# A deeper u lead in layer 1, GpSimd splits in halves beside G, and adaLN tiles beside layer 0's routing

## The chip, the cores and the metric

One core of a Trainium2 chip runs the whole program. The metric is the device time of one execution in microseconds (us), as the median of several runs. The engines are PE (TensorE, matrix products), DVE (VectorE), ACT (ScalarE), POOL (GpSimd) and the DMA queues, of which SP issues most. Each engine works off its own list of instructions strictly in order; semaphores make one engine wait for another.

## The reference

The program is a two-layer transformer trunk for 256 latent and 256 context tokens of width 1024. Each layer has adaLN modulation, four token mixers, and an expert layer (PEER), which is the part that the change touches:

```
mod_lat = (jax.nn.silu(c) @ w_mod[l] + b_mod[l])[:, None, :]     # adaLN, six vectors per layer
...
def peer_ffn(h, w_q, subkeys, u, v):                             # 16384 experts of one neuron
    q = (x_t @ w_q).reshape(t, PEER_HEADS, 2, PEER_QDIM // 2)
    s = jnp.einsum('thpd,hpnd->thpn', q, subkeys)                # routing: scores of 2 x 128 keys
    s_top, i_top = lax.top_k(s, kk)
    ...
    best, pos = lax.top_k(cand, kk)                              # 16 experts per head and token
    g = jax.nn.softmax(best, axis=-1)
    a = jax.nn.gelu(jnp.einsum('td,thkd->thk', x_t, u_sel))
    return jnp.einsum('thk,thkd->td', g * a, v_sel)
```

Layer 0 treats latent and context tokens, layer 1 only the 256 latent ones.

## The kernel before

The expert layer doesn't gather. It multiplies the tokens with all 16384 rows of u, in 128 tiles of 128 experts, and later with all rows of v. A dense matrix G (experts x tokens), made from the routing's result, holds the weight of every expert for every token and is zero where an expert wasn't chosen. Layer 0 does this for 384 of its tokens and gathers rows for the last 128 (class `Chosen`, the indirect DMAs); layer 1 does it for all 256.

Products are made to float32 precision from split operands: a tile `raw` is loaded, ACT copies it into a rounded `w_hi` (L144), and DVE or POOL subtracts to get `w_lo` (L145). Three products, hi by hi, hi by lo and lo by hi, are added in PSUM (L183 for u, L806 for v). `lo_engine` gives a share of the subtractions, `self.share`, to POOL and the rest to DVE. There are two `w_hi` and two `w_lo` buffers, and 4 (layer 0) or 5 (layer 1) `raw` buffers.

A layer's expert part has these stages, in program order:

1. **Routing** (`route`): 16 products with w_q, scores, top-16 searches on DVE, one softmax (`g`, ACT's exponential at L984). Then `ahead()` emits the first `LEAD0` u tiles (`u_step`), whose results are parked in SBUF (`park`, ACT's gelu at L753). The routing's result is then transposed on PE (L998) into `i1T`, `i2T` and `gT`; these transposes are told to stand behind the last matmul of `ahead()`:

```
        last = ahead()
        for src, dst in ((e2[0], i1T), (e2[1], i2T), (g, None)):
            ps = self.psum("big")
            with self.tc.issue_after(last):
```

2. **Lead** (first loop of `experts`): the u tiles from `LEAD0` to `LEAD`, and between them the steps that make G (`g_step`, 48 in layer 0, 32 in layer 1). A step is three DVE operations on float16 (p2 L763, pg L767, p1 L771, shown as p, pg and p), 16 small products on PE (L779), ACT copies into `stage` (L782) and every other step a DMA of 1 MB to G in DRAM. The last `LEAD1` u tiles come after the last step.
3. **Experts** (second loop): G is read back (`gr`, L789), and for each of 128 tiles j the parked u result is multiplied with its rows of G (L795), split, and multiplied with v tile j (`v_step`). While u tiles are left, one follows each v step. So there are 128 minus `LEAD` steps with v and u, then `LEAD` steps with v alone.

In layer 0 the lead loop also calls `fill_in()`, which takes the next of 25 small steps that compute a part of layer 1's adaLN: 20 tiles of w_mod (a 512 KB load and 8 matmuls, L292) and five layouts (an ACT copy, four transposes on PE at L301, two or three tiny DVE operations at L305, L306 and L310).

The order of instructions on each engine isn't the program order. A scheduler plays the program through with modelled times and fixes each engine's list by that; the constants above and the place of a call in the program are what it starts from.

Of the kernel before, what the change touches and what calls it, by code (L numbers as in the profile page):

```python
# [8 lines left out]
F32 = mybir.dt.float32  # L9
# [26 lines left out]

GB = 16
GI = 8
LEAD = [40, 60]

LEAD0 = [17, 12]
LEAD1 = [6, 6]


# [10 lines left out]
MRAW1 = 5  # L55
MB = [2, 3]
SHARE = [0.64, 0.888, 0.75]
PSH = [[1.0, 0.65, 0.6], [1.0, 0.3, 0.3]]
GATHERS = [0.3, 2.35]
SHL = [0.3, 0.181]  # L60
DIRECT = 7
# [7 lines left out]
class K:  # L69
    def __init__(self, tc, a, out):  # L70
        self.tc, self.nc, self.a, self.out = tc, tc.nc, a, out
        self.n_lo = 0.0
        self.fresh = False
        self.gates = []
        self.rows = None
        self.fill = []
        self.share = 0.5


    def rsqrt(self, ss, inv_n):  # L80
# [57 lines left out]
                self.r = self.rsqrt(s["ps"][:, :n // 128], 1.0 / D)  # L138
        return step

    def split(self, hi, lo, src, lo_engine=None):

        nc = self.nc
        nc.scalar.activation(hi, src, AF.Copy)  # L144
        (lo_engine or nc.vector).tensor_sub(lo, src, hi.bitcast(F32))  # L145

    def lo_engine(self, work=1.0):

# [6 lines left out]
    def weights(self, src, n=1024, tag="w", whole=False):  # L155
        nc, pool = self.nc, self.wp if tag == "w" else self.wk
        raw = self.raw() if tag == "w" else pool.tile([128, n], F32, name="b_raw", tag="braw", bufs=BB)
        nc.sync.dma_start(raw, src)
        hi = pool.tile([128, n], F32R, name="w_hi", tag=tag + "hi", bufs=2 if tag == "w" else BB)
        lo = pool.tile([128, n], F32R, name="w_lo", tag=tag + "lo", bufs=2 if tag == "w" else BB)  # L160
        self.split(hi, lo, raw, self.lo_engine())
        return (hi, lo, raw) if whole else (hi, lo)

    def raws(self, name, n):
# [559 lines left out]
    def peer(self):  # L724
# [4 lines left out]
        tc, nc, a, l = self.tc, self.nc, self.a, self.l  # L729
        n = DENSE[l]  # L730
        nt = n // 128
        self.chosen = None
        lead = LEAD[l]
        with self.pool("pe") as hp, tc.tile_pool(name="gd", bufs=1, space=bass.MemoryType.DRAM) as dp:
# [13 lines left out]
            def u_step(j):  # L748
                hi, lo = self.weights(a["u"][l, j])
                ps = self.psum("acc")[:, :n]  # L750
                end = self.mm(ps, hi, lo, lambda kt: P[0][:, kt, :n], lambda kt: P[1][:, kt, :n], DT)
                park[j] = hp.tile([128, n], F32, name="park", tag="park", bufs=lead + 1)
                nc.scalar.activation(park[j], ps, AF.Gelu)  # L753
                if self.chosen:
                    self.chosen.behind = end.ins
                return end.ins
# [81 lines left out]
            def phase(i, ns):  # L838

                self.share, self.n_lo = PSH[l][i], 0.0  # L840
                if self.chosen:
# [4 lines left out]
            with self.pool("route") as wk:  # L846
                own = None
                if self.chosen:
                    own = wk.tile([128, DT, 128], F32, name="own")
                P[:] = self.norm_mod(wk, hp, NB, LAT if self.last else ALL, 1, n, own)  # L850
                self.share = SHARE[2]


                def ahead():
                    self.share, self.n_lo = PSH[l][0], 0.0
                    return [u_step(j) for j in range(LEAD0[l])][-1]

                self.route(wk, n, *P, own, i1T, i2T, gAB, ahead)
            with self.pool("rows") as p:
# [4 lines left out]
    def experts(self, l, lead, n, gp, vp, u_step, g_step, g_read, v_step, v_end, phase):  # L864

        tb = TB
        with self.pool("g") as p:
            gp.append(p)
            gather = phase(0, lead)
            k, k0, k1 = 0, LEAD0[l], lead - LEAD1[l]  # L870
            for i in range(k0, lead):
                u_step(i)
                gather()
                self.fill_in()
                while k < n // tb and k < (i + 1 - k0) * n / (tb * (k1 - k0)):
                    g_step(k * tb)
                    k += 1
            self.fill_in(99)
        with self.pool("v") as p:
            vp.append(p)  # L880
            g_read(0)
            gather = phase(1, 128 - lead)
            for j in range(128):
                if j == 128 - lead:
                    gather = phase(2, lead)
                if j % GI == 0 and j + GI < 128:
                    g_read(j + GI)
                v_step(j)
                if j + lead < 128:
                    u_step(j + lead)  # L890
                gather()
            if self.chosen:
                self.chosen.finish()
            v_end()
# [356 lines left out]
```

## Time and profile before

| | before |
|---|---|
| median of 3 runs | 3302.24 us (3292.46 to 3308.22) |
| profiled execution, its own time | 3292.48 us |
| span from first to last instruction | 3290.7 us |
| mean granted TensorE clock | 0.962 |
| layer 0: G made, first v product | 826.6 to 1027.4, 1051.8 us |
| layer 1: G made, first v product | 2530.8 to 2704.0, 2724.0 us |

The times inside the program are microseconds from the span's start. A view by windows tells how long each engine was busy in a stretch; the timeline lists single instructions, with the idle time before each and what ended it in brackets.

### The profile page before, as it was taken

The page shows a single profiled execution, that of the slowest core. Times are in us where ns is not written, and L with a number is a line of the kernel's source. Part 1 is how long each engine was busy: PE and PEld are TensorE (multiplying, and loading weights), DVE is VectorE, ACT ScalarE, POOL GpSimd, SP SyncE. Part 2 cuts the span into 40 slices and gives each one's busy share as a digit, 9 for nine tenths or more (in the row PEclk, how much of TensorE's full clock was granted, in tenths as well). Part 3 has the DMA queues.
Part 4 walks back from the last instruction along what each step waited for, and adds up shares of the span by engine and source line. Part 5 has one row for each costly group of instructions (what it writes and reads, how often), then busy time and mean ns, then how long its engine had stood idle before and what let it go on. Part 6 is the DMA issues. An engine that isn't in the chain of part 4 may idle for free. (4 is left out here: it accounts for less than half of the span.)

```text
span 3290.7 us, 49451 instructions
## 1 busy us (share of the span) xinstructions
PE 3074.5 (93%) x19063; PEld 2707.9 (82%) x19063; DVE 2361.8 (72%) x4092; ACT 1366.5 (42%) x2166; POOL 1527.7 (46%) x814
## 2 busy tenths in 40 slices
PE   7999999898887899999999997999987889999998
PEld 5877777797776799988899886788987888999887
DVE  5465453799986888787888875456599988666655
ACT  4454443323443333333333333355543544444454
POOL 1111322135443688877888862245345663222221
PEclk9999999899988999999999997899988999999999
DMA  7331332222668988888888865333434669666564
GB/s 253 106 103 46 112 113 98 72 91 90 249 231 273 306 304 293 292 279 299 295 295 282 274 209 175 116 122 130 149 120 135 211 216 303 211 215 209 191 194 133
DMA packets 251292, 641.21 MB, mean 195 GB/s; under 512 B 20016, under 2 KB 107696, under 8 KB 245936
## 3 DMA queue, kind: packets, MB, share of 16 engines
q1 hardware_dynamic: 208432, 461.88, 42.9%
q0 software_dynamic: 36864, 134.23, 11.7%
q10 hardware_dynamic: 5760, 41.95, 3.4%
q8 instruction: 149, 2.44, 0.3%
q14 instruction: 87, 0.71, 0.1%
HBM read 594.99 MB, written 42.99 MB: 194 GB/s over the span
## 5 line engine op out<-in xcount | busy, mean ns | idle before, releaser
L145 POOL TENSOR_TENSOR w_lo<-raw,w_hi 128x1024 fp32r<-128x1024 f32 x387 | 1008.7, 2611 | 1306.8 <-ACT w_hi L144 959.4
L144 ACT ACTIVATE w_hi<-raw 128x1024 fp32r<-128x1024 f32 x664 | 703.7, 1060 | 1168.4 <-PE ps_acc L183 468.1
L183 PE MATMUL ps_acc<-hhi,w_hi 128*128 128x256 f32 (+2 forms) x3136 | 988.5, 333 | 51.4 <-ACT park L753 19.8
L183 PE MATMUL ps_acc<-hlo,w_hi 128*128 128x256 f32 (+2 forms) x3136 | 964.6, 326 | 0.5 <-DVE hlo L355 0.5
L183 PEld LDWEIGHTS ps_acc<-hhi,w_hi 128*128 128x128 f32 x3136 | 611.4, 195 | 94.4 <-ACT park L753 21.2
L183 PEld LDWEIGHTS ps_acc<-hlo,w_hi 128*128 128x128 f32 x3136 | 608.8, 194 | 27.8 <-DVE hlo L355 1.5
L183 PE MATMUL ps_acc<-hhi,w_lo 128*128 128x256 f32 (+2 forms) x3136 | 576.5, 324 | 32.7 <-POOL w_lo L145 22.6
L183 PEld LDWEIGHTS ps_acc<-hhi,w_lo 128*128 128x128 f32 x3136 | 496.1, 192 | 62.2 <-POOL w_lo L145 26.7
L145 DVE TENSOR_TENSOR w_lo<-raw,w_hi 128x1024 fp32r<-128x1024 f32 x277 | 359.2, 1297 | 238.8 <-ACT w_hi L144 156.8
L806 PE MATMUL ps_big<-w_hi,whi 128*128 128x512 f32 x1280 | 341.6, 394 | 17.2 <-ACT w_hi L144 17.2
L806 PE MATMUL ps_big<-w_lo,whi 128*128 128x512 f32 x1280 | 332.9, 390 | 3.3 <-DVE w_lo L145 3.1
L806 PE MATMUL ps_big<-w_hi,wlo 128*128 128x512 f32 x1280 | 335.2, 391 | 0.0
L806 PEld LDWEIGHTS ps_big<-w_lo,whi 128*128 128x128 f32 x1280 | 239.4, 188 | 54.5 <-DVE w_lo L145 4.9
L806 PEld LDWEIGHTS ps_big<-w_hi,wlo 128*128 128x128 f32 x1280 | 240.9, 188 | 52.4
L806 PEld LDWEIGHTS ps_big<-w_hi,whi 128*128 128x128 f32 x1280 | 234.8, 189 | 57.3 <-ACT w_hi L144 18.9
L1100 DVE SCALAR_TENSOR_TENSOR ch<-row,cg,ch 128x1024 f32<-128x1024 f32 x127 | 232.3, 1829 | 68.7 <-DMA row<-in_v_rows,cx 67.6
L795 DVE TENSOR_TENSOR park<-park,gr 128x384 f32<-128x384 f32 (+1 forms) x256 | 232.8, 938 | 65.1 <-ACT park L753 37.6
L1094 DVE SCALAR_TENSOR_TENSOR row<-row,ch 128x1024 f32<-128x1024 f32 x128 | 211.8, 1670 | 77.2 <-DMA row<-in_u_rows,cx 76.7
L145 DVE TENSOR_TENSOR wlo<-park,whi 128x256 fp32r<-128x256 f32 (+1 forms) x214 | 203.0, 951 | 48.0 <-ACT whi L144 47.9
L1067 POOL DMA_INDIRECT row<-in_u_rows,cx x128 | 181.6, 1419 | 34.0 <-issue 18.3
L1067 POOL DMA_INDIRECT row<-in_v_rows,cx x128 | 174.8, 1366 | 30.5 <-issue 22.4
L753 ACT ACTIVATE park<-ps_acc 128x384 f32<-128x384 f32 (+1 forms) x256 | 110.6, 432 | 120.5 <-PE ps_acc L183 117.9
(223 smaller groups left out, 3469.6 us busy)
## 6 DMA issues: line engine op xcount, KB each, us to landing
raw<-in_u SPq DMA_DIRECT2D x256, 512.0 KB
raw<-in_v SPq DMA_DIRECT2D x256, 512.0 KB
raw<-in_w_mod SPq DMA_DIRECT2D x96, 512.0 KB
G<-stage ACTq DMA_DIRECT2D x40, 1024.0 KB
raw<-in_w_gate SPq DMA_DIRECT2D x64, 512.0 KB
gr<-G SPq DMA_DIRECT2D x16, 1536.0 KB
raw<-in_w_in SPq DMA_DIRECT2D x40, 512.0 KB
raw<-in_w_q SPq DMA_DIRECT2D x32, 512.0 KB
```

Source lines behind the costliest of these rows:

```text
L144: nc.scalar.activation(hi, src, AF.Copy)
L145: (lo_engine or nc.vector).tensor_sub(lo, src, hi.bitcast(F32))
L183: end = nc.tensor.matmul(ps, w[:, kt * 128:kt * 128 + 128], x(kt), start=i == 0, stop=i == 3 * nk - 1)
L753: nc.scalar.activation(park[j], ps, AF.Gelu)
L795: nc.vector.tensor_mul(w3, w3, g)
L806: m = nc.tensor.matmul(vacc[0][t][d], x[:, t * 128:t * 128 + 128], y[:, d * 512:d * 512 + 512], start=first, stop=end)
L1067: dma = nc.gpsimd.indirect_dma_start(out=row, out_offset=None, in_=self.k.a["u_rows" if i < SLOTS else "v_rows"], in_offset=bass.IndirectO ...
L1094: nc.vector.scalar_tensor_tensor(row, row, 1.0, self.h, op0=OP.mult, op1=OP.mult, accum_out=self.dot[:, s:s + 1])
L1100: nc.vector.scalar_tensor_tensor(self.y, row, self.g[:, s:s + 1], self.y, op0=OP.mult, op1=OP.add)
```

## The change

Layer 1 gets 84 u tiles in its lead instead of 60, and 28 of them, instead of 12, are emitted in `ahead()`. For the tiles of `ahead()` every subtraction stays on POOL (share 1.0), but in layer 1's lead loop POOL's share falls from 1.0 to 0.55. While a lead loop runs, in both layers, a subtraction that goes to POOL is cut into two of 512 columns. And `ahead()` now calls `fill_in()` after each u tile, so that 17 of layer 0's 25 adaLN steps are emitted there (in layer 1 there is nothing to fill in).

```
-LEAD = [40, 60]
-LEAD0 = [17, 12]
+LEAD = [40, 84]
+LEAD0 = [17, 28]
-PSH = [[1.0, 0.65, 0.6], [1.0, 0.3, 0.3]]
+PSH = [[1.0, 0.65, 0.6], [0.55, 0.3, 0.3]]
...
-    def split(self, hi, lo, src, lo_engine=None):
+    def split(self, hi, lo, src, lo_engine=None, pieces=1):
         nc = self.nc
         nc.scalar.activation(hi, src, AF.Copy)
-        (lo_engine or nc.vector).tensor_sub(lo, src, hi.bitcast(F32))
+        n = lo.shape[1] // pieces
+        for i in range(pieces):
+            c = slice(i * n, i * n + n)
+            (lo_engine or nc.vector).tensor_sub(lo[:, c], src[:, c], hi[:, c].bitcast(F32))
...
-        self.split(hi, lo, raw, self.lo_engine())
+        e = self.lo_engine()
+        self.split(hi, lo, raw, e, self.pieces if e is nc.gpsimd else 1)
...
                 def ahead():
-                    self.share, self.n_lo = PSH[l][0], 0.0
-                    return [u_step(j) for j in range(LEAD0[l])][-1]
+                    self.share, self.n_lo = 1.0, 0.0
+                    for j in range(LEAD0[l]):
+                        last = u_step(j)
+                        self.fill_in()
+                    return last
...
             k, k0, k1 = 0, LEAD0[l], lead - LEAD1[l]
+            self.pieces = 2
             for i in range(k0, lead):
...
             self.fill_in(99)
+            self.pieces = 1
```

No instruction of PE, ACT or SP is added or removed. Of the subtractions of full tiles, 12 move from POOL to DVE, and 53 of those that stay on POOL become 106 halves.

What moves is seen in the lists of the engines. First ACT in layer 1, from the softmax's exponential (`g<-g`) to the copies of the transposed routing (`i1T`, `i2T`, `gT`). Before (the numbers of tiles are shown, since the rows read alike without them):

```order
L984 ACTIVATE g_23229<-g_23229 128x256
L753 ACT_TABLE_LOAD
L753 ACTIVATE park_23685<-ps_acc_23660 128x256
L144 ACTIVATE w_hi_23836<-raw_23834 128x1024
L753 ACTIVATE park_23745<-ps_acc_23720 128x256
L144 ACTIVATE w_hi_23896<-raw_23894 128x1024
L753 ACTIVATE park_23805<-ps_acc_23780 128x256
L144 ACTIVATE w_hi_23929<-raw_23927 128x1024
L1002 ACTIVATE i1T_21968<-ps_big_23632 128x256
```

and in the changed kernel (L995 is L984, L145 is L144, L759 is L753 and L1013 is L1002 of before):

```order
L995 ACTIVATE g_23252<-g_23252 128x256
L759 ACT_TABLE_LOAD
L759 ACTIVATE park_23686<-ps_acc_23661 128x256
L145 ACTIVATE w_hi_23756<-raw_23754 128x1024
L759 ACTIVATE park_23719<-ps_acc_23694 128x256
...
L145 ACTIVATE w_hi_24267<-raw_24265 128x1024
L759 ACTIVATE park_24181<-ps_acc_24156 128x256
L1013 ACTIVATE i1T_21991<-ps_big_24183 128x256
```

Three parks stand between the exponential and the first transposed copy before, 16 after; ahead of the exponential 12 parks and 13 `w_hi` copies stand behind the routing's last `q`, in both. The first half of the added tiles is not placed beside the searches but behind the softmax.

Second, POOL in layer 1, from the routing's last conversion (`xf`) to its third subtraction in the expert stage (`wlo<-park`). Before:

```order
L940 CAST xf<-idx 128x32
L145 TENSOR_TENSOR w_lo<-raw,w_hi 128x1024 x46
L145 TENSOR_TENSOR wlo<-park,whi 128x256
L145 TENSOR_TENSOR w_lo<-raw,w_hi 128x1024 x21
L145 TENSOR_TENSOR wlo<-park,whi 128x256
```

and in the changed kernel:

```order
L951 CAST xf<-idx 128x32
L149 TENSOR_TENSOR w_lo<-raw,w_hi 128x1024 x15
L149 TENSOR_TENSOR w_lo<-raw,w_hi 128x512 x60
L149 TENSOR_TENSOR wlo<-park,whi 128x256
L149 TENSOR_TENSOR w_lo<-raw,w_hi 128x1024 x20
```

So 30 of the 56 lead tiles are split on POOL, in 60 halves; the rest are on DVE, 21 of them between its first and last operation for G. On PE, 45.75 u tiles lie between the first and the last product for G, where 33.5 lay before; 3.25 (before 3.2) lie between the transposes and the first of these products, and 6.7 between the last one and the first v product, in both.

Third, the SP queue at the end of layer 0's lead (`raw<-in_u`, `raw<-in_v` and `raw<-in_w_mod` are loads of tiles, `gr<-G` the reads of G). Before:

```order
L158 DMA raw<-in_u 128x1024
L289 DMA raw<-in_w_mod 128x1024 x2
L789 DMA gr<-G 128x24x128 x2
L158 DMA raw<-in_v 128x1024
L158 DMA raw<-in_u 128x1024
```

and in the changed kernel:

```order
L162 DMA raw<-in_u 128x1024 x16
L162 DMA raw<-in_v 128x1024
L162 DMA raw<-in_u 128x1024
L162 DMA raw<-in_v 128x1024
L162 DMA raw<-in_u 128x1024
L162 DMA raw<-in_v 128x1024
L162 DMA raw<-in_u 128x1024
L162 DMA raw<-in_v 128x1024
L795 DMA gr<-G 128x24x128 x4
```

Four v tiles and three u tiles are now asked for ahead of the first read of G, and no tile of w_mod stands near it. Of the 20 tiles of w_mod, 14 and three layouts now stand on PE ahead of layer 0's transposes, and ACT has 6 parks instead of 4 between layer 0's exponential and its transposed copies.

## Rows read from the trace of the kernel before

**Rows 1.** The page's busy times: engine, busy us, share of the span, instructions.

```profile
PE 3074.5 (93%) x19063; PEld 2707.9 (82%) x19063; DVE 2361.8 (72%) x4092; ACT 1366.5 (42%) x2166; POOL 1527.7 (46%) x814
```

**Rows 2.** Windows: stretch, busy us of the engines, granted clock, DMA share, GB/s.

```profile
2530.00:2704.00 174.00, 147.92 (x1392) 144.06 (x1391) 169.91 (x98) 84.66 (x138) 109.83 (x38) 0.96 0.59 203
...
2724.00:3111.00 387.00, 385.35 (x2463) 350.83 (x2462) 264.07 (x281) 185.91 (x274) 107.15 (x44) 1.00 0.71 225
3111.00:3273.00 162.00, 162.00 (x717) 134.07 (x715) 85.26 (x95) 78.85 (x115) 41.07 (x22) 1.00 0.55 177
...
827.00:1027.00 200.00, 165.96 (x1523) 151.81 (x1521) 181.40 (x172) 82.65 (x140) 81.75 (x29) 0.91 0.65 237
...
1052.00:1110.00 58.00, 47.72 (x215) 41.75 (x216) 44.10 (x57) 15.77 (x21) 33.54 (x21) 0.91 1.06 339
```

**Rows 3.** Timeline of layer 1's softmax, ACT (start, us, instruction, idle before).

```profile
2517.53 0.42 ACT L984 ACTIVATE g<-g 128x256 f32<-128x256 f32 x1 [8.15 <-DVE g L983]
...
2527.65 0.38 ACT L1002 ACTIVATE i1T<-ps_big 128x256 f16<-128x256 f32 x1
```

**Rows 4.** The same stretch on PE.

```profile
2519.69 0.58 PE L183 MATMUL ps_acc<-hhi,w_hi 128*128 128x256 f32 x1 [6.28 <-ACT park L753]
```

**Rows 5.** Timeline of DVE at the start of layer 1's G.

```profile
2530.79 0.68 DVE L763 TENSOR_TENSOR p<-iotaT,i2T 128x1024 f16<-128x1024 f16 x1
2531.39 3.43 DVE L771 TENSOR_TENSOR p<-iota,i1T 128x1024 f16<-128x1024 f16 x1
...
2544.33 1.21 DVE L767 TENSOR_TENSOR pg<-p,gAB 128x2048 f16<-128x2048 f16 x1
```

**Rows 6.** The same stretch on POOL.

```profile
2531.28 2.45 POOL L145 TENSOR_TENSOR w_lo<-raw,w_hi 128x1024 fp32r<-128x1024 f32 x1 [1.02 <-ACT w_hi L144]
```

**Rows 7.** Groups by line, 2530 to 2704: busy us, mean ns, idle before.

```profile
L145 POOL TENSOR_TENSOR w_lo<-raw,w_hi 128x1024 fp32r<-128x1024 f32 x38 | 112.5, 2965 | 64.8 <-ACT w_hi L144 42.9 <-PE ps_acc L183 14.2 <-ACT stage L782 7.8
...
L767 DVE TENSOR_TENSOR pg<-p,gAB 128x2048 f16<-128x2048 f16 x32 | 56.2, 1760 | 2.2 <-PE ps_big L779 2.2
...
L779 PE MATMUL ps_big<-p,pg 128*128 128x128 f16 x512 | 40.7, 237 | 26.1 <-DVE p L771 22.1 <-DVE pg L767 4.0
```

**Rows 8.** Timelines of DVE and of PE at the end of layer 1's lead.

```profile
2700.91 1.21 DVE L771 TENSOR_TENSOR p<-iota,i1T 128x1024 f16<-128x1024 f16 x1
...
2724.03 1.09 PE L806 MATMUL ps_big<-w_hi,whi 128*128 128x512 f32 x4
```

**Rows 9.** Groups of the whole run: POOL's half-wide split, DVE's full split.

```profile
L145 POOL TENSOR_TENSOR w_lo<-b_raw,w_hi 128x512 fp32r<-128x512 f32 x24 | 31.4, 1313 | 76.7 <-ACT w_hi L144 67.9 <-PE ps_big L607 8.3 <-issue 0.3
...
L145 DVE TENSOR_TENSOR w_lo<-raw,w_hi 128x1024 fp32r<-128x1024 f32 x277 | 359.2, 1297 | 238.8 <-ACT w_hi L144 156.8 <-PE ps_acc L183 74.9 <-PE ps_big L806 4.1
```

**Rows 10.** Timelines of POOL and DVE where a half-wide split met a DVE split.

```profile
53.76 1.29 POOL L145 TENSOR_TENSOR w_lo<-b_raw,w_hi 128x512 fp32r<-128x512 f32 x1 [0.33 <-ACT w_hi L144]
...
54.15 1.45 DVE L145 TENSOR_TENSOR w_lo<-b_raw,w_hi 128x512 fp32r<-128x512 f32 x1
```

**Rows 11.** Groups by line, 827 to 1045 (layer 0's lead).

```profile
L767 DVE TENSOR_TENSOR pg<-p,gAB 128x2048 f16<-128x2048 f16 x48 | 66.2, 1383 | 17.2 <-PE ps_big L779 17.2
...
L144 ACT ACTIVATE w_hi<-raw 128x1024 fp32r<-128x1024 f32 x21 | 22.1, 1056 | 26.5 <-DMA raw<-in_u 23.9 <-PE ps_acc L183 2.2 <-ACT stage L782 0.4
...
L292 PE MATMUL ps_big<-raw,cv 128*32 128x128 f32 x320 | 15.0, 306 | 0.0
```

**Rows 12.** Timelines of SP, DVE and PE where layer 0's G is read back.

```profile
1034.59 5.36 SPq L789 DMA_DIRECT2D gr<-G  x2
1040.04 5.54 SPq L158 DMA_DIRECT2D raw<-in_v  x1
...
1044.03 3.84 DVE L795 TENSOR_TENSOR park<-park,gr 128x384 f32<-128x384 f32 x8 [2.59 <-DMA gr<-G]
...
1051.75 1.65 PE L806 MATMUL ps_big<-w_hi,whi 128*128 128x512 f32 x3 [10.81 <-ACT w_hi L144]
```

More of the change, by code (lines that the diff above doesn't have):

```diff
@@ L878, in experts @@
             self.fill_in(99)
+            self.pieces = 1
         with self.pool("v") as p:
```

## The prediction

> **What bounds the kernel now.** The page comes first: PE is busy for 93% of the span [rows 1], so a change can win only where PE idles. The windows show where that is. While layer 1's experts run, PE has no gap, with v and u (387 us for 68 steps) or v alone (162 us for 60) [rows 2]. While layer 1's G is made, 2530 to 2704, PE is busy for 148 of 174 us and DVE for 170; in layer 0's lead PE for 166 and DVE for 181 of 200 [rows 2]. So DVE sets the pace of both leads, and the change moves PE work into them.
>
> The second thing to see is what DVE's time in layer 1's lead is made of. Alone, p2 takes 0.68 us, and pg and p1 1.21 us each; an operation starts some 0.08 us before the one in front of it ends [rows 5, 8]. But a p1 of 1.21 us took 3.43 when a POOL split had begun 0.1 us before it [rows 5, 6]. From the first p2 (2530.8) to the end of the last p1 (2702.1) [rows 5, 8] it is 171.3 us. The 32 steps alone are 32 x (0.60 + 1.13 + 1.13) = 91.5, and DVE waited 2.2 for PE [rows 7]; the other 77.6 us are stalls beside 38 POOL splits [rows 7], 2.04 us for each, 0.83 of a split's 2.45 [rows 6].
>
> The Trainium skill's page "SBUF — State Buffer", section "Who interferes with whom", says that a DVE instruction with two SBUF inputs and a GpSimd instruction that reads SBUF exclude each other, and that whoever issues first keeps the port for its whole instruction. By that rule the DVE splits that the change adds stand under the same lock, and the two engines' times would add up in full: 91.5 + 25.6 + 56 x 1.31 + 2.2 = 192.7 us on DVE in the stage worked out below, and v at 2784, where the share of 0.83 gives 180.3 us and, as far as DVE goes, v at 2772. The trace agrees with the lock [rows 5, 6], and with its holding for a DVE split too [rows 10].
>
> **Layer 1: what leaves the experts.** A step with v and u takes 387/68 = 5.69 us, one with v alone 162/60 = 2.70 [rows 2], so a u tile is worth 2.99 us there. 24 of them leave: -71.8 us.
>
> **Layer 1: the first 16.** ACT stood 8.15 us in front of the softmax's exponential, which waits for DVE's searches, and ran it at 2517.5; PE idled 6.28 us behind ACT until 2519.7 [rows 3, 4]. In the changed lists 12 parks stand ahead of the exponential, as before, so nothing more can run beside the searches, and PE's gaps up to 2519.7 stay. Behind it stand 16 parks instead of 3, and the transposes come behind the last of these tiles. 13 more tiles at 2.99 us push the transposes back by 38.9 us: the first copy from 2527.7 to 2566.6, the first p2 from 2530.8 to 2569.7 [rows 3, 5]. For these 39 us DVE has nothing to do. PE can hold 2.99 us there, since ACT's copy takes 1.06 us per tile [rows 11] and POOL's split 2.45 [rows 6]. If the tiles did fit beside the searches, this cost would be nothing; the list speaks against it.
>
> **Layer 1: while G is made.** DVE: 91.5 us for the steps; 21 splits, by their mean of 1.30 less 0.08 [rows 9], 25.6; and the stalls beside the 28 other tiles of this stage (of 3.25 + 45.75), split on POOL in 56 halves. The trace has no half of this tile in this stage. Its nearest row is the POOL split of 512 columns, 1.31 us [rows 9]; begun at 53.76, it held a DVE split back that began at 54.15 and took 1.45 us, where a DVE split of twice the width takes 1.30 [rows 9, 10]. So a half stalls DVE until its own end and not longer. I take 0.83 x 1.31 = 1.09 per half, 61 us; the bounds are a free half and a full 1.31 us (73). With 2.2 of waiting that is 180.3 us, and the last p1 ends at 2750. PE: 46 tiles x 2.99 + 40.7 for the products of G [rows 7] = 178 us. It starts after 3.25 tiles behind the transposes, at 2577, and ends no earlier than 2755.
>
> So the two engines are now equally loaded, and what counts is how often one waits for the other. PE waited 26.1 us for p1 and pg in this stage [rows 7]; with DVE no longer far behind I take 8, bounds 0 and 26. The last product for G comes at 2763 (2755 to 2781). From the last p1 to the first v product it was 21.9 us [rows 8], some 20.7 from the last G product, and 6.7 u tiles lie in it in both kernels. So v starts at 2784 (2776 to 2802) instead of 2724.0: +60 us (+52 to +78). Layer 1: 60 - 71.8 = -12 us (-20 to +6).
>
> **Layer 0.** Four terms. (1) Between its softmax and its transposes stand 6 parks instead of 4. A u tile here has 384 columns instead of 256, so 1.5 x 2.99 = 4.5 us; about four tiles of w_mod at 15.0/20 = 0.75 [rows 11] come with them: +12 us on the start of G. (2) In the lead DVE waited 17.2 us for PE, and ACT 23.9 us for loads of u [rows 11], which share four buffers with the tiles of w_mod. 14 of the 20 leave this stage; I take half of the wait as won, -9 (0 to -17). The halves change little: 22 tiles here instead of 21. (3) The first v tile was asked for at 1040.0, behind two reads of G, and PE stood 10.81 us until its copy came, though the multiplication with G began at 1044.0 [rows 12]. Now it is loaded ahead: v can start about 6 us sooner (0 to -8). (4) From 1052 to 1110 the DMA engines are full (share 1.06, 339 GB/s) and PE is busy for 47.7 of 58 us [rows 2]. The 3.5 MB asked for earlier are 10 us of that traffic; I take -3 (0 to -10). Together -6 us, from +12 to -23.
>
> The gathers of layer 0 move by a few places in DVE's list; they are a fixed number and lie in stretches where PE has no gap. Costed at nothing.
>
> **The sum.** -12 - 6 = -18 us. The profiled execution (3292.48 us, a span of 3290.7 and 1.8 around it) would become 3274. It lies 9.8 under the median of the runs, whose spread is 16 us, so for the median I take 18 from 3302.24: 3284 us. A measurement of this kernel can tell a difference of about 0.5%, 16.5 us, from none.
>
> **Rivals.**
>
> *More is won (chance 0.18).* PE stays at its own pace in layer 1's lead (-20) and layer 0 gets back most of its waits (-16): 3266 us. For it: the halves let p1 and pg in sooner, and PE's 26.1 us of waits all came from DVE. Against it: both engines are full at once, and each works in order.
>
> *The hole isn't paid back (chance 0.22).* The 39 us in which DVE stands still are a loss on the engine that set the pace, and the 26 us of waits remain or layer 0's later G outweighs its prefetch: layer 1 at -6 to +6, layer 0 at 0 to +6, about 3301 us. For it: the exponential's place in ACT's list.
>
> *Slower: DVE's splits wait for ACT (chance 0.12).* 21 splits now stand in DVE's list between the steps of G, and each holds everything behind it until its `w_hi` is there; `w_hi` needs a buffer that PE frees two tiles earlier. Over the run the 277 DVE splits waited 238.8 us [rows 9], 0.86 each. At that rate DVE would end 21 x 0.86 = 18 us later than 2750, which is inside the bounds above. From 1.2 us each (DVE at 2775, v at 2796) layer 1 wins nothing. At 2.5 us DVE ends at 2803 and v starts at 2824, +100 - 72 = +28, and with layer 0 at -6 the kernel is at 3324 us. Against it: POOL's waits for `w_hi` here, 42.9 us over 38 splits [rows 7], are 1.1 each, and POOL's list holds nothing else.
>
> **How the numbers follow.** The forecast, -18 us, has a chance of 0.48, with its own range from 3270 to 3296. I give it 0.55 to lie beyond -16.5 us. Faster by over 0.5%: 0.48 x 0.55 + 0.17 of the first rival = 0.43. Within 0.5%: 0.22 + 0.21 + 0.01 + 0.01 of the last = 0.45. Slower: 0.12 with what the runs' spread can add. The range goes from 3264, the low end of the first rival, to 3308, which is the nothing-won case with the spread of the runs; about 2 in 10 lie outside.
>
> **What would show it.** In the changed profile: PE's gap before layer 1's exponential still there, at about the same time; then 16 u tiles without a gap, DVE idle for about 39 us, and the first p2 of layer 1 some 39 us later against the stage's start; p2, pg and p1 stalled by 1.1 us instead of 2.2 at a time; DVE at about 180 us from first p2 to last p1; PE's wait for p1 and pg down from 26; v started 60 us later, and 44 steps with v and u. In layer 0: transposes about 12 us later, and no 10.8 us gap before the first v product. It is wrong if p2 starts where it did, which would mean that the tiles found room beside the searches; if a half stalls DVE as long as a whole split; or if DVE's w_lo rows show idle time of over 1.2 us each in layer 1's lead.

## The result and the profile after

The changed kernel takes 3262.45 us (median of 4 runs, 3257.93 to 3263.62) against 3297.35 for the kernel before beside it: a ratio of 0.9897, 95% interval 0.9875 to 0.9918. Run again later on another chip it took 3271.26 against 3297.97, 0.9917 (0.9899 to 0.9936). So it is faster by 1.0%, or some 30 us; 18 were forecast, and 3262.45 lies 1.5 us below the range.

The profiled execution took 3257.93 us, 34.6 less than that of before. The busy times of its page, as in [rows 1]:

```profile
PE 3069.0 (94%) x19063; PEld 2701.3 (83%) x19063; DVE 2312.9 (71%) x4101; ACT 1367.5 (42%) x2166; POOL 1531.1 (47%) x858
```

Windows as in [rows 2]: layer 1 from the exponential to the first v product, its G stage, its experts with v and u and with v alone, then layer 0's G stage and the 15 us ahead of its first v product.

```profile
2514.30:2759.80 245.50, 239.92 (x2190) 237.23 (x2191) 191.03 (x158) 131.98 (x214) 140.25 (x74) 0.99 0.66 224
2562.00:2734.00 172.00, 168.78 (x1611) 166.33 (x1610) 168.25 (x119) 95.65 (x156) 95.38 (x50) 1.00 0.67 233
2760.00:3012.00 252.00, 250.68 (x1599) 227.36 (x1599) 180.57 (x225) 121.49 (x178) 68.89 (x28) 1.00 0.78 246
3012.00:3239.00 227.00, 227.00 (x1003) 187.80 (x1001) 123.17 (x134) 111.82 (x163) 57.34 (x31) 1.00 0.58 181
843.50:1053.80 210.30, 170.05 (x1418) 161.05 (x1417) 196.42 (x177) 87.65 (x143) 113.04 (x57) 0.89 0.62 224
1057.00:1072.00 15.00, 0.09 (x1) 0.09 (x1) 1.25 (x3) 1.06 (x3) 0.00 (x0) 0.60 0.81 242
```

In layer 1's G stage PE is now busy for 169 of 172 us, where it was 148 of 174. DVE is as full as before (168), but with more tiles beside it. In layer 0 the same stage is longer than before, and PE still idles for 40 us in it.

Layer 1's softmax on ACT, and PE behind it, as in [rows 3, 4]:

```profile
2514.34 0.42 ACT L995 ACTIVATE g<-g 128x256 f32<-128x256 f32 x1 [8.14 <-DVE g L994]
...
2559.36 0.38 ACT L1013 ACTIVATE i1T<-ps_big 128x256 f16<-128x256 f32 x1
```
```profile
2516.50 0.58 PE L189 MATMUL ps_acc<-hhi,w_hi 128*128 128x256 f32 x1 [6.27 <-ACT park L759]
...
2521.41 0.28 PE L189 MATMUL ps_acc<-hhi,w_hi 128*128 128x256 f32 x1
...
2558.85 0.60 PE L1009 MATMUL ps_big<-ident,e 128*128 128x128 f32 x4
```

The gap before the exponential stayed, 6.27 us on PE. From 2521.41 to the transposes lie 13 u tiles: 37.44 us, 2.88 each. One more lies between 2516.50 and 2521.41.

DVE and POOL at the start of layer 1's G, as in [rows 5, 6], and DVE at its end:

```profile
2556.35 1.22 DVE L149 TENSOR_TENSOR w_lo<-raw,w_hi 128x1024 fp32r<-128x1024 f32 x1 [31.22 <-ACT w_hi L145]
...
2562.06 0.68 DVE L769 TENSOR_TENSOR p<-iotaT,i2T 128x1024 f16<-128x1024 f16 x1
...
2566.67 2.31 DVE L149 TENSOR_TENSOR w_lo<-raw,w_hi 128x1024 fp32r<-128x1024 f32 x1
2568.91 2.31 DVE L773 TENSOR_TENSOR pg<-p,gAB 128x2048 f16<-128x2048 f16 x1
...
2731.11 2.31 DVE L777 TENSOR_TENSOR p<-iota,i1T 128x1024 f16<-128x1024 f16 x1
```
```profile
2565.77 4.37 POOL L149 TENSOR_TENSOR w_lo<-raw,w_hi 128x512 fp32r<-128x512 f32 x2 [3.91 <-ACT w_hi L145]
```

DVE's hole is there (31.22 us in front of one split), and an operation of 1.21 us that meets a half takes 2.31 instead of 3.43.

The groups by line of that stage, 2562 to 2734, as in [rows 7]:

```profile
L149 POOL TENSOR_TENSOR w_lo<-raw,w_hi 128x512 fp32r<-128x512 f32 x50 | 95.4, 1930 | 75.1 <-ACT w_hi L145 75.1
L777 DVE TENSOR_TENSOR p<-iota,i1T 128x1024 f16<-128x1024 f16 x32 | 55.3, 1728 | 0.0
L773 DVE TENSOR_TENSOR pg<-p,gAB 128x2048 f16<-128x2048 f16 x32 | 51.5, 1610 | 3.7 <-PE ps_big L785 3.6
L769 DVE TENSOR_TENSOR p<-iotaT,i2T 128x1024 f16<-128x1024 f16 x32 | 38.2, 1195 | 0.0
L785 PE MATMUL ps_big<-p,pg 128*128 128x128 f16 x496 | 37.7, 229 | 1.6 <-DVE p L777 1.2 <-DVE pg L773 0.5
L149 DVE TENSOR_TENSOR w_lo<-raw,w_hi 128x1024 fp32r<-128x1024 f32 x22 | 32.1, 1458 | 0.0
```

PE's wait for p and pg fell from 26.1 us to 1.6. This is the row that the gain hangs on. PE's work for this stage lies a little later than DVE's, from its first product for G to its last. Below are the rows of both, and the window between them:

```profile
2568.86 0.83 PE L785 MATMUL ps_big<-p,pg 128*128 128x128 f16 x10
...
2739.13 1.20 PE L785 MATMUL ps_big<-p,pg 128*128 128x128 f16 x16
```
```profile
2568.90:2740.30 171.40, 168.18 (x1613) 165.73 (x1612) 161.92 (x113) 96.56 (x157) 95.59 (x52) 1.00 0.68 237
```

### The profile page after: what moved, and what is told of

Read it like the earlier page. It is cut to its first block, busy times and chain, and to the rows that moved or that the text cites. A ratio compares the mean times of both kernels' runs of the same rounds, so it can differ in the third digit from the quotient of the medians.

```text
span 3256.1 us, 49522 instructions
## 1 busy us (share of the span) xinstructions
PE 3069.0 (94%) x19063; PEld 2701.3 (83%) x19063; DVE 2312.9 (71%) x4101; ACT 1367.5 (42%) x2166; POOL 1531.1 (47%) x858
## 3 DMA queue, kind: packets, MB, share of 16 engines
q1 hardware_dynamic: 208432, 461.88, 43.9%
## 5 line engine op out<-in xcount | busy, mean ns | idle before, releaser
L149 POOL TENSOR_TENSOR w_lo<-raw,w_hi 128x1024 fp32r<-128x1024 f32 (+1 forms) x428 | 1012.8, 2375 | 1262.9 <-ACT w_hi L145 946.9
L145 ACT ACTIVATE w_hi<-raw 128x1024 fp32r<-128x1024 f32 x664 | 703.9, 1061 | 1193.0 <-PE ps_acc L189 505.4
L189 PEld LDWEIGHTS ps_acc<-hlo,w_hi 128*128 128x128 f32 x3136 | 604.9, 193 | 26.1 <-issue 0.9
L149 DVE TENSOR_TENSOR w_lo<-raw,w_hi 128x1024 fp32r<-128x1024 f32 x289 | 376.0, 1302 | 295.5 <-ACT w_hi L145 206.6
L812 PE MATMUL ps_big<-w_hi,whi 128*128 128x512 f32 x1280 | 340.9, 393 | 15.1 <-ACT whi L145 15.1
L1111 DVE SCALAR_TENSOR_TENSOR ch<-row,cg,ch 128x1024 f32<-128x1024 f32 x127 | 244.1, 1922 | 63.4 <-DMA row<-in_v_rows,cx 61.9
L801 DVE TENSOR_TENSOR park<-park,gr 128x384 f32<-128x384 f32 (+1 forms) x256 | 213.7, 870 | 50.1 <-DMA gr<-G 30.7
L149 DVE TENSOR_TENSOR wlo<-park,whi 128x256 fp32r<-128x256 f32 (+1 forms) x211 | 181.5, 862 | 32.6 <-ACT whi L145 32.3
L1078 POOL DMA_INDIRECT row<-in_v_rows,cx x128 | 174.3, 1362 | 31.0 <-issue 23.3
L759 ACT ACTIVATE park<-ps_acc 128x384 f32<-128x384 f32 (+1 forms) x256 | 110.6, 432 | 108.4 <-PE ps_acc L189 104.1
```

The lines of the kernel that those rows point to most:

```text
L149: (lo_engine or nc.vector).tensor_sub(lo[:, c], src[:, c], hi[:, c].bitcast(F32))
L189: end = nc.tensor.matmul(ps, w[:, kt * 128:kt * 128 + 128], x(kt), start=i == 0, stop=i == 3 * nk - 1)
L801: nc.vector.tensor_mul(w3, w3, g)
L812: m = nc.tensor.matmul(vacc[0][t][d], x[:, t * 128:t * 128 + 128], y[:, d * 512:d * 512 + 512], start=first, stop=end)
L1078: dma = nc.gpsimd.indirect_dma_start(out=row, out_offset=None, in_=self.k.a["u_rows" if i < SLOTS else "v_rows"], in_offset=bass.IndirectO ...
L1111: nc.vector.scalar_tensor_tensor(self.y, row, self.g[:, s:s + 1], self.y, op0=OP.mult, op1=OP.add)
```

## The experiments

Theory A: the gain is layer 1's. 24 u tiles leave experts in which PE is full for a lead in which PE idled, and they fit there only because DVE is relieved by POOL's smaller share. Layer 0's edits come to nothing, and the halves add little. The rivals are in the expectations. The table shows layer 1 in ten kernels, in us, read from the timelines of each profile (in numbers 4 and 10 to 13 the sum lies within 4 us of the changed kernel's). "Experts" runs from the first v product to the start of the last ones on `w_hi`; "stalls" is the time that p2, pg and p1 took over 0.68, 1.21 and 1.21 us, with the number of POOL pieces beside them:

| kernel | exp. to first p2 | first p2 to last p1 | last p1 to v | experts | sum | stalls (pieces) |
|---|---|---|---|---|---|---|
| before | 13.3 | 171.3 | 21.9 | 547.5 | 754.0 | 77.1 (37) |
| changed | 47.8 | 171.4 | 26.4 | 477.6 | 723.1 | 45.8 (50) |
| layer 1 alone | 48.4 | 171.4 | 26.4 | 478.4 | 724.6 | 45.9 (50) |
| layer 0 alone | 13.0 | 171.4 | 21.8 | 546.8 | 753.0 | 75.3 (37) |
| no halves | 48.5 | 174.0 | 26.2 | 477.8 | 726.6 | 41.4 (25) |
| share 1.0 | 48.5 | 190.6 | 29.0 | 477.5 | 745.6 | 97.8 (91) |
| twelve ahead | 15.2 | 200.2 | 35.6 | 476.5 | 727.4 | 31.5 (62) |
| quarters | 48.0 | 174.4 | 28.0 | 477.7 | 728.2 | 35.9 (101) |
| depth only | 47.6 | 196.6 | 24.7 | 477.8 | 746.7 | 93.3 (47) |
| share and halves only | 15.1 | 154.9 | 26.0 | 546.0 | 742.0 | 33.2 (39) |

**1. Layer 1's edits alone.** Relative to the changed kernel:

```
-                        self.fill_in()
...
-            self.pieces = 2
+            self.pieces = 1 + l
```

> Layer 1's edits alone (28 tiles ahead, 84 in the lead, POOL's share 0.55, halves in layer 1); layer 0 as before. Theory A, the gain is layer 1's, 24 u tiles moved into a lead in which PE idled, and layer 0's edits come to nothing: about 34 us under the kernel before, the first v product of layer 1 some 36 us later against the exponential and the experts of layer 1 some 70 us shorter; first p2 to last p1 in layer 0 at about 197 us as before. Rival B, layer 0's adaLN move carries a good part: no more than 15 to 20 us under the kernel before.

3267.77 us, 0.9916 of before (0.9887 to 0.9946). Layer 1 is 29.4 us shorter from the exponential on, and the total 27 us (34 expected). Theory A.

**2. Layer 0's edits alone.** `LEAD`, `LEAD0` and `PSH` as before, and

```
-            self.pieces = 2
+            self.pieces = 2 - l
```

> Layer 0's edits alone (adaLN steps beside the routing, halves in layer 0's lead); layer 1 as before. Theory A: within 8 us of the kernel before; first p2 to last p1 in layer 0 about 210 us against 197, the first v product some 18 us behind the last p1 against 28, layer 0's experts some 9 us shorter. Rival B: 15 us or more under the kernel before.

3297.44 us, 1.000 (0.998 to 1.002). Rival B is out. Layer 0's experts came out 2 us shorter, not 9.

**3. No halves.** `self.pieces = 1` in both layers.

> The whole change, but every POOL split in one piece. Theory A: a stall is as long as the piece, so in layer 1 some 22 stalls of 2.2 us take the place of 44 of 1.1, 48 us either way; layer 1's G keeps its length within 8 us, layer 0's loses about 13 us of DVE time, and the kernel is 0 to 12 us under the changed one. Rival C, the halves are what made layer 1's lead dense: PE's wait for p1 and pg in layer 1's lead goes back above 15 us, and the kernel is 10 us or more over the changed one.

3265.79 us, 0.9920 (0.9894 to 0.9946): no difference from the changed kernel that can be told. In the profile layer 1 is 3.5 us longer, and the stalls come to about the same sum, 41.4 us on 25 pieces instead of 45.8 on 50. PE waited 1.1 us for p and pg, so rival C is out. But layer 0's G stage didn't get shorter either (208.7 us), against theory A.

**4. Halves in layer 1 only.** `self.pieces = 1 + l`.

> The whole change, but halves in layer 1 only. Theory A: layer 0's DVE is stalled 12 times by 2.2 us instead of 37 times by 1.1, first p2 to last p1 in layer 0 back to about 197 us from 210, the kernel some 10 us under the changed one. Rival D, layer 0's lead is longer because of the tiles and adaLN steps that moved, not because of the halves: no difference from the changed kernel, and 210 us stay.

3259.68 us, 0.9911 (0.9879 to 0.9943). Layer 0's G stage took 210.1 us, with 43.9 us of stalls on 23 whole splits, where the halves gave 40.5 on 44. My guess that the halves lengthened it fell; rival D holds. It names moved tiles and moved adaLN steps, and no run separates these two.

**5. POOL's share back at 1.0, in halves.** `PSH[1][0]` is 1.0.

> The whole change, but POOL's share in layer 1's lead loop stays at 1.0, in halves. Theory A, the share is what relieves DVE: 49 tiles beside G are some 98 halves, 0.9 stalls of 1.1 us for each, so DVE needs 91.5 + 97 = 188 us from first p2 to last p1 against 171 in the changed kernel; PE waits for p and pg again (15 us or more), and the kernel is 14 to 22 us over the changed one. Rival E, the share doesn't matter because PE paces the stage anyway: 171 to 175 us and no difference.

3285.71 us, 0.9959 (0.9942 to 0.9977); 190.6 us from first p2 to last p1, in which DVE idled 0.8 us. Theory A, and rival E is out. One part missed: PE waited only 7.8 us for p and pg (15 expected), and 10.2 for `w_lo`, nearly all of it POOL's.

**6. Twelve tiles ahead.** `LEAD0 = [17, 12]`, `LEAD` as changed.

> The whole change, but 12 u tiles ahead of layer 1's transposes instead of 28, so 72 in the lead loop. Theory A, PE is dense from the exponential to the first v product in any case, so the hole in DVE's work is free: exponential to first p2 back to 13 us, first to last p1 some 206 us, exponential to first v product 245 us as in the changed kernel (within 4), no difference in time. Rival F, the hole of 39 us in which DVE stands still is a loss that is paid for: 10 us or more under the changed kernel. Rival G, with more tiles between them p and pg hold PE up again: over 5 us slower than the changed kernel.

3268.09 us, 0.9910 (0.9892 to 0.9929). The hole is gone, and nothing is won: from the exponential to the first v product 250.9 us against 245.5. PE's busy time there is the same, its idle time 11.0 us instead of 5.6, as this kernel's window of that stretch shows:

```profile
2517.00:2767.90 250.90, 239.94 (x2207) 236.99 (x2206) 186.19 (x172) 133.12 (x214) 123.89 (x77) 1.00 0.67 225
```

DVE's idle time didn't go away: it now stands still for 45 us inside the stage, as its groups from first p2 to last p1 show:

```profile
L773 DVE TENSOR_TENSOR pg<-p,gAB 128x2048 f16<-128x2048 f16 x32 | 49.1, 1538 | 20.8 <-PE ps_big L785 20.8
L149 DVE TENSOR_TENSOR w_lo<-raw,w_hi 128x1024 fp32r<-128x1024 f32 x25 | 33.0, 1321 | 24.6 <-ACT w_hi L145 24.6
```

So the hole cost nothing, and rival F is out. The 5.4 us are a little over what A allowed; rival G's loss in total isn't measured.

**7. Only the depth.** Share 1.0, no halves, layer 0 as before.

> Only the depth: 84 u tiles in layer 1's lead, 28 ahead of the transposes; share 1.0, no halves, layer 0 as before. Theory A: 49 whole POOL splits beside G at 2.04 us of stall each, DVE 91.5 + 100 + 2 = 194 us against 171; the first v product some 60 to 65 us later against the exponential, the experts 70 shorter; 5 to 10 us under the kernel before. Rival H, depth alone does it: 25 us or more under the kernel before.

3292.53 us, 0.9981 (0.9965 to 0.9998). First the window of this kernel from the exponential to the first v product, then PE's products for G in the same stretch:

```profile
2525.80:2794.70 268.90, 245.61 (x2190) 242.99 (x2191) 206.88 (x132) 132.53 (x214) 191.40 (x70) 0.96 0.60 204
```
```profile
L785 PE MATMUL ps_big<-p,pg 128*128 128x128 f16 x512 | 41.5, 240 | 19.6 <-DVE p L777 15.1 <-DVE pg L773 4.5
```

The tiles are in the lead, but PE waits 19.6 us for p and pg between them, and the lead grows by nearly all that the experts lose. Rival H is out.

**8. Only the share and the halves.** `LEAD` and `LEAD0` as before, layer 0 as before.

> Only the relief of DVE: 60 and 12 tiles as before, share 0.55 and halves in layer 1's lead, layer 0 as before. Theory A: 37 tiles beside G, some 17 of them on DVE (1.22 us each) and 20 in 40 halves of 0.9 x 1.1 us: DVE 91.5 + 21 + 40 + 2 = 154 us instead of 171, so layer 1's first v product comes 13 to 17 us sooner against the exponential, the experts are as long as before, and the kernel is 13 to 17 us under the kernel before. Rival I, relief without more tiles is worth nothing, since PE's list sets the end of the lead: under 5 us.

3284.75 us, 0.9954 (0.9933 to 0.9974). Rival I is out. DVE's stage shrinks by 16.4 us as expected, and 4.1 of it are lost behind the last p1: PE's last product for G ends 4.1 us behind it, where it was 1.3 before. That its waits for `w_lo`, which it didn't have before, put PE that far behind is likely but not shown. PE's rows for the exponential to the first v product:

```profile
L189 PE MATMUL ps_acc<-hhi,w_lo 128*128 128x256 f32 x370 | 55.2, 291 | 9.8 <-POOL w_lo L149 6.0 <-DVE w_lo L149 3.8
L785 PE MATMUL ps_big<-p,pg 128*128 128x128 f16 x512 | 39.5, 232 | 7.1 <-DVE p L777 6.6 <-DVE pg L773 0.5
```

By the sums of the table, depth alone gives 7.3 us, share and halves alone 12.0, both 29.4 to 30.9: some 10 us come only from the two together, by one profile of each.

**9. Quarters in layer 1.** `self.pieces = 2 + 2 * l`.

> The changed kernel, but layer 1's POOL splits beside G come in quarters of 256 columns. Theory A, a stall is as long as the piece that holds the port: twice as many stalls of half the length, 0.5 to 0.65 us, the sum of the stalls again about 46 us (42 to 55) and 171 us from first p2 to last p1; no difference in time. Rival J, the cut itself relieves DVE: the sum falls below 35 us. Rival K, each POOL instruction has a price of its own: the sum rises over 60 us and the stage with it.

3278.48 us, 0.9951 (0.9928 to 0.9973). The stalls fell to 35.9 us, between A and rival J, and yet the G stage took 3.0 us longer. DVE waited 11.0 us for PE there (3.7 in the changed kernel), and POOL was busy for 137.7 us instead of 95.4. That POOL held PE up is likely but not shown: PE's waits for `w_lo` only rose from 1.6 to 3.8 us. POOL's group there:

```profile
L149 POOL TENSOR_TENSOR w_lo<-raw,w_hi 128x256 fp32r<-128x256 f32 x101 | 137.7, 1393 | 37.6 <-ACT w_hi L145 28.2 <-PE ps_big L785 9.4
```

A quarter takes 1393 ns here, more than a half takes undisturbed (1313 [rows 9]). Layer 1 lost 5.1 us by the table. The rest of the loss in total lies in layer 0's experts, where the program is that of the changed kernel; it is told of at the end.

**10 and 11. Share 0.55 in layer 0's lead too,** and with it 42 tiles there and whole pieces in layer 0.

```
-PSH = [[1.0, 0.65, 0.6], [0.55, 0.3, 0.3]]
+PSH = [[0.55, 0.65, 0.6], [0.55, 0.3, 0.3]]
```

> The changed kernel, but POOL's share is 0.55 in layer 0's lead too. Theory A, what counts in a lead is DVE's time while it paces G: of 22 tiles beside G some 10 go to DVE (12 us) and 12 stay in 24 halves, whose stalls come to 22 us instead of 40, so first p2 to last p1 in layer 0 falls from 210 to 200 to 206 us and the kernel gains 4 to 10 us. Rival L, layer 0's lead is held by loads and PE as much as by DVE: no change from 210, or no change in the kernel's time.

> As the last one, with two u tiles more in layer 0's lead (42) and whole POOL splits there. Theory A: PE idles 40 us beside layer 0's G, two tiles of 384 columns (4.4 us each) find room in it and leave the experts: 4 to 12 us under the changed kernel. Rival L: no difference from the changed kernel.

3255.17 us, 0.9882 (0.9856 to 0.9907), and 3265.23, 0.9912 (0.9887 to 0.9937). With the share alone layer 0's G stage fell to 198.2 us, a little below the expected 200. With two more tiles it took 206.3, and layer 0's experts were no shorter (914.7 against 914.5): nothing won, so the second expectation of A failed. The run changes the depth and the pieces at once and doesn't tell which of them it was. Its profile shows where the 8 us went: DVE waited 10.7 us for gathered rows in this stage, where it waited 2.5 in number 10. The rows of number 10, then of number 11:

```profile
L1105 DVE SCALAR_TENSOR_TENSOR row<-row,ch 128x1024 f32<-128x1024 f32 x13 | 17.9, 1380 | 2.5 <-DMA row<-in_u_rows,cx 2.5
```
```profile
L1105 DVE SCALAR_TENSOR_TENSOR row<-row,ch 128x1024 f32<-128x1024 f32 x13 | 16.0, 1231 | 10.7 <-DMA row<-in_u_rows,cx 10.7
```

**12 and 13. The changed kernel and number 10 on one chip.**

> The changed kernel itself, on the same chip as the next run. Theory A: 0.988 to 0.992 of the kernel before, as layer 1's edits alone gave; layer 0's first p2 to last p1 about 210 us.

> The changed kernel with share 0.55 in layer 0's lead too, beside the changed kernel on the same chip. Theory A, DVE paces layer 0's lead: first p2 to last p1 again about 198 us, and the 12 us reach the end, 7 to 14 us under the changed kernel. Rival L, they are lost again in layer 0's experts, which are full of DMA at their start: within 4 us of the changed kernel.

3271.26 us, 0.9917 (0.9899 to 0.9936), and 3256.14, 0.9868 (0.9844 to 0.9892): 15 us apart (7 to 14 expected). In the two profiles the stage takes 210.0 and 198.2 us and the whole span differs by 12.2, so the 12 us reach the end, and DVE's time there was on the path. This version beats both kernels: 1.3% under the one before. The windows of this stage, first the changed kernel's, then number 13's:

```profile
840.20:1050.20 210.00, 170.01 (x1418) 161.03 (x1417) 198.50 (x177) 87.19 (x142) 112.14 (x57) 0.89 0.62 224
```
```profile
843.50:1041.80 198.30, 167.50 (x1418) 157.32 (x1417) 191.42 (x187) 87.60 (x142) 74.53 (x37) 0.91 0.65 236
```

## Why the prediction was too cautious

**The step that failed is layer 1's start of v, forecast at +60 us.** Against the exponential it came 39.0 us later (245.5 against 206.5), and layer 1 won 30.9 us instead of 12, more than the 20 that the prediction allowed at most. The mechanisms were there; the terms were too large. The sum went by PE: its first product for G at 2577, 178 us of work, 8 of waiting, and 20.7 to v.

- *The first 16.* The first product for G came 54.5 us behind the exponential, 59.5 forecast. I took 13 more tiles at 2.99 us, counted by the parks in ACT's list. On PE it was 12 (14 tiles from 2516.50 to the transposes, where before just under two lay between 2519.69 and them), and a dense one takes 2.88 us, so the transposes came 34.9 us later and not 38.9.
- *PE's work while G is made*: 168.2 us, forecast 178. This is the largest term. A tile was priced at what it is worth in the experts, 2.99; 45.75 tiles at 2.88 are 5.8 us less than 46 at 2.99. The other 4 us aren't told apart; G's products were priced at 40.7 us of busy time in a stretch with a granted clock of 0.96, and here they took 39.0 at 1.00.
- *Waiting in it*: 3.2 us, of which 1.6 for p and pg, forecast 8.
- *From the last product for G to v*: 19.5 us, forecast 20.7.

These are 5 + 10 + 5 + 1 of the 21 us by which the start of v was off. The lower bound, +52, had no waiting in it; that v came sooner still is owed to PE's earlier start and its own time.

DVE's time stood beside this sum, which took from it only the 8 us of waiting. It was too large as well: 171.4 us, forecast 180.3. Measured it is 91.5 for the steps + 30.3 for 22 splits (32.1 less 0.08 each) + 45.8 of stalls + 3.7 of waiting = 171.3. The stalls were mis-sized: 50 halves at 0.92, not 56 at 1.09 (61 us). The Trainium skill, "SBUF — State Buffer", "Who interferes with whom", has such instructions of DVE and GpSimd exclude each other, the later one blocked for the whole of the other. The trace agrees for the single stall: 2.31 less 1.21 is 1.10 us, within a half's own 1.31 [rows 9]. It doesn't bear out the 192.7 us worked out from that rule, in which each half costs DVE its whole length: 44 stalls beside 50 halves cost 45.8 us. A half takes POOL 1930 ns there.

The first rival ("more is won") was the right one for layer 1, and still too small. That the depth needs the relief, which the sum took as given, is shown by numbers 5, 7 and 8. That the time missed the range by 1.5 us only is in part luck: the kernel before, put at 3302.24 us, took 3297.35 beside the changed one, and on the second chip the changed kernel took 3271.26.

**What leaves the experts** was right: 69.9 us measured, 71.8 forecast.

**The hole** was rightly put on DVE (the first p2 34.5 us later) and rightly let into the sum only through PE; number 6 shows that it costs nothing by itself. **DVE's splits waiting for ACT**, the slower rival, did not happen: their idle time in this stage is 0.0. (In number 6 it was 24.6 us, about 1 us each.)

**Layer 0**: forecast -6 us, measured nothing (number 2, whose interval is 6.6 us to either side). Term by term, before against changed: (1) from the last `q` to the first p2 it is 7 us longer, +12 forecast. (2) The G stage is 13.4 us longer where I had 9 shorter. (3) The first v product comes 18.2 instead of 28.3 us behind the last p1, -10 for -6, but not in the way forecast: PE's gap in front of it didn't go, it grew from 10.81 to 15.14 us, and now waits for G to be read back (the first rows below). What went is most of PE's work between the last p1 and this gap, 17.5 us before and 3 after. (4) The experts are perhaps 5 us shorter, 918 on the mean of eight profiles with the adaLN move (910 to 925) against 923 of four without it (920 to 925), -3 forecast. Term (2) had the wrong sign, and numbers 1 and 2 show why. First PE and DVE ahead of the first v product in the changed kernel, then groups of the G stage in number 1 (layer 0 as before) and in number 2 (layer 0 changed):

```profile
1071.91 2.50 PE L812 MATMUL ps_big<-w_hi,whi 128*128 128x512 f32 x5 [15.14 <-ACT whi L145]
```
```profile
1070.75 3.37 DVE L801 TENSOR_TENSOR park<-park,gr 128x384 f32<-128x384 f32 x7 [15.90 <-DMA gr<-G]
```
```profile
L773 DVE TENSOR_TENSOR pg<-p,gAB 128x2048 f16<-128x2048 f16 x48 | 63.8, 1333 | 16.1 <-PE ps_big L785 16.1
...
L189 PE MATMUL ps_acc<-hhi,w_lo 128*128 128x384 f32 x160 | 35.2, 360 | 7.8 <-POOL w_lo L149 7.8
...
L145 ACT ACTIVATE w_hi<-raw 128x1024 fp32r<-128x1024 f32 x19 | 20.0, 1056 | 25.6 <-DMA raw<-in_u 23.0 <-PE ps_acc L189 2.2 <-ACT stage L788 0.4
L1104 DVE SCALAR_TENSOR_TENSOR row<-row,ch 128x1024 f32<-128x1024 f32 x9 | 12.8, 1427 | 0.6 <-DMA row<-in_u_rows,cx 0.6
```
```profile
L773 DVE TENSOR_TENSOR pg<-p,gAB 128x2048 f16<-128x2048 f16 x48 | 70.4, 1470 | 9.1 <-PE ps_big L785 9.1
...
L189 PE MATMUL ps_acc<-hhi,w_lo 128*128 128x384 f32 x192 | 42.3, 359 | 6.7 <-POOL w_lo L149 6.7
...
L145 ACT ACTIVATE w_hi<-raw 128x1024 fp32r<-128x1024 f32 x24 | 25.4, 1060 | 39.3 <-PE ps_acc L189 25.0 <-POOL w_lo L149 10.0 <-DMA raw<-in_u 2.9
L1105 DVE SCALAR_TENSOR_TENSOR row<-row,ch 128x1024 f32<-128x1024 f32 x13 | 16.8, 1297 | 0.3 <-DMA row<-in_u_rows,cx 0.3
```

The waits went as forecast: 23.0 us for loads of u to 2.9, DVE's 16.1 for PE to 9.1. But the room was taken by four more u tiles (192 matmuls are 24 tiles, 160 are 20) and by four more of the gathers' row operations on DVE, 4.0 us, which I had "costed at nothing". DVE paces this stage, and beside the added tiles its stalls grew from 25.8 to 43.3 us. (The prediction had 22 tiles for 21 in this lead.) Why 20 steps were stalled beside 23 whole splits in number 4 and only 12 beside 19 before isn't settled.

## What to carry to other kernels

Moving work into an engine's idle time pays only as far as the engine that paces that stage has room: here depth alone gave 7 us, relief alone 12, both 30, so price the two together, and count the terms from the lists of both busy engines, at the price that they have in that stage (PE's 168.2 + 3.2, DVE's 91.5 + 30.3 + 45.8 + 3.7). A tile's worth in another stage isn't its price here: 2.99 against 2.88 us. A hole in a side engine cost nothing (number 6) while the engine that bounds the kernel was dense across it. Steps that "lie in stretches where PE has no gap" must be looked up again in the changed lists: the four row operations that came into DVE's full stage were not free.

## What the runs showed of the hardware

PE's busy time for the same work isn't fixed. From the exponential to the first v product it was busy for 239.92 us in the changed kernel, with 5.6 us idle at a granted clock of 0.99; in number 7 for 245.61 us, with 23.3 idle at 0.96 and the same 2190 records; in number 5 for 246.34, with 21.8 idle at 0.98. Some 6 us come on top of the waits. It goes with the granted clock rather than with the idle time, since number 6 idled 11.0 us at 1.00 and was busy for 239.94; how much of it is the clock isn't settled.

Cutting POOL's pieces shortened each stall, but hardly their sum. At share 0.55 a stalled step lost at most 2.2 us beside whole splits (number 3), 1.1 beside halves and 0.6 beside quarters (number 9). But 21 steps were stalled by 25 whole splits, 44 by 50 halves and 66 by 101 quarters, and the sums are 41.4, 45.8 and 35.9 us. What relieved DVE was taking splits off POOL: from share 1.0 to 0.55, both in halves, the sum fell from 97.8 to 45.8 us and the stage from 190.6 to 171.4.

Layer 0's experts took 911.8 us in the first profile of the changed kernel and 923.2 in the second. PE's rows, first and second:

```profile
L189 PE MATMUL ps_acc<-hhi,w_hi 128*128 128x384 f32 x696 | 236.0, 339 | 7.5 <-ACT w_hi L145 7.5
```
```profile
L189 PE MATMUL ps_acc<-hhi,w_hi 128*128 128x384 f32 x696 | 236.9, 340 | 11.7 <-ACT w_hi L145 11.7
```

The same list waited 4.2 us longer there for `w_hi`, which is 4 of the 11 us; totals of one kernel differ by 10 us and more, so the stages were compared too.
